# First mixer's small loads, the routing's order, narrow second blocks, and 18 chunk buffers

## The chip, the core and the metric

The kernel runs on one core of one Trainium2 chip. Time is the device time of one execution in microseconds (us); three executions of the kernel before took 1806.77, 1803.26 and 1806.77 us, median 1806.77. PE is TensorE, DVE is VectorE, ACT is ScalarE, POOL is GpSimd and SP is the engine that issues the transfers of the weights here.

## The reference, cut to what matters

Two transformer blocks follow each other on 256 tokens of width 1024 in float32. What the change touches:

```python
# first block
z = rms_norm(h, attn_norm) @ w_in                     # q, k, v, u
h = h + concat(diff_attention(q, k, v), pool_mixer(u)) @ w_out
h = h + moe(rms_norm(h, ffn_norm))                    # 32 experts, 4 for each token
h = h + sigmoid(rms_norm(h, ple_gate_norm) @ w_ple_gate) * rms_norm(p @ w_ple_proj, ple_post_norm)
# moe: logits = xn @ w_router + b_router; top 4; softmax of these; for expert e
gt = minimum(xb @ w_gate[e] + b_gate[e], 7.0); up = clip(xb @ w_up[e] + b_up[e], -7.0, 7.0)
y = ((up + 1.0) * (gt * sigmoid(1.702 * gt))) @ w_down[e] + b_down[e]
# second block: window attention and a gated recurrence, then
h = h + hierarchical_moe(rms_norm(h, norm2_w_2))      # 4 groups of 8 experts, 2 for each token
```

In the first mixture each matrix of an expert is 1024 x 1024 (4 MiB), in the second 1024 x 512. With the inputs of the reference expert 0 of the first mixture gets 73 tokens, and no other expert of it more than 64.

## The kernel before

All weights, some 655 MB, are streamed once. `specs()` lists them as chunks of 1 MiB in the order of their use, and `w_issue` (line 154) issues them from SP in that order, as soon as a buffer is free in the pools that are open: 7 buffers always (`wp`), 4 more in pool `m1_xa` from the end of the first mixer on, and 6 more in the first mixture (`NX[False] = (4, 6)`), 17 in all. A buffer comes free with `w_done`, when the last reader of its chunk has finished.

**Mixers.** A dense product takes its weights in two halves: `piece_emit` lets ACT write the rounded half `w_hi` and DVE the rest `w_lo` into a ring of four, and PE multiplies both (tile `lin`). The first mixer runs `lin_first` and three `lin_tok` (q and k, v, u), with the attention and the pool beside them, and then the product with `w_out`. `attend_pool` asks at its start for the small loads `aux`, `bands`, `wpool` and `bias_sb` (line 560), and after the second product for `wr_sb` (line 611), the two routers' matrices, which DVE multiplies by the gains. After the pool it splits the experts' biases: ACT copies `bias_sb` to `bias` (line 91) and DVE subtracts to get the lower half. In this middle part the scheduler sets the order on each engine, so these instructions don't stand where the code has them.

**Routing** (`route`, both mixtures) is written out in order. For each half of the tokens ("tile" 0 and 1) `added` adds the product to `h_res`, `squares` and `factor` give the norm's factor `rr`, `keep` writes the normed tokens in two halves, `xth` on ACT and `xtl` on DVE, `turn` transposes `h_res` into a `w_hi` room, `logits` multiplies with `wr_sb`, `choose` picks the experts on DVE (`le` to `sel`), and `place` counts them on PE (`po`). `weights` then makes the slots `posm`, the gates, and the counts `cnt`, on which the mixtures' first count loads, and so the next chunks, wait. `one_hots` makes `P`, with which `gather` collects the tokens of four (or eight) experts.

**First mixture** (`all_experts`). For each expert `gate`, `up` and `down` multiply 4 chunks each with the first 64 tokens of the expert; `product` then opens `tc.If(cnt > 64)` (line 1583), and its body `extra` does the same for the tokens 64 to 127, with tiles of 512 columns in two groups of 64. `more`, for an expert with over 128 tokens, stands at expert 24 (line 1768). The gate of the per-layer embedding has its first chunks (`w_ple_gate`, columns 0 to 511, two chunks) ahead of expert 31's `w_up`; they are split at expert 30 into four kept rooms of pool `m1_xa`. `mixer2` begins with the product of these and with the remaining `w_ple_gate`.

Of the kernel before, what the change touches and what calls it, by code (L numbers as in the profile page):

```python
# [10 lines left out]
F32 = mybir.dt.float32  # L11
# [67 lines left out]
class Prog:  # L79
# [346 lines left out]
    def specs(self):  # L426
# [34 lines left out]
        def mixture(second):  # L461
            for e in range(33):
# [16 lines left out]
        self.w_until[False] = len(s)  # L479
        cols(A["w_ple_gate"][0], 512, 1024, PK_PLE)  # L480
# [62 lines left out]
    def attend_pool(self, ph, xh, xl):  # L543

        nc, tc = self.nc, self.tc
        if True:
# [7 lines left out]
            wpool = sb.tile([128, 4, 128], F32, name="wpool")  # L554
# [85 lines left out]
            for _ in side:  # L640
                pass
            return acc
# [153 lines left out]
    def mixer2(self):  # L796
        nc, tc = self.nc, self.tc
        with ExitStack() as ph:
# [7 lines left out]
            with tc.tile_pool(name="b_ple", bufs=2, reuse_waits="tile") as gp:  # L806
                ws = self.p_q
                self.pieces_begin(sp, 29, 0)
                self.norm_tr(self.h[:, 0], 0, xh, xl)
                ss = self.small.tile([128, 2, 2], F32, name="gss")  # L810
# [24 lines left out]
                for t in range(2):  # L835
                    for n in range(4):
# [6 lines left out]
                        if t == 0 and n == 3 or t and n < 2:  # L843
                            self.piece_emit()
# [375 lines left out]
    def route(self, ph, xh, xl, accs):  # L1220
# [17 lines left out]
        def turn(t):  # L1238
            x = r["xT"][t] = self.sp.tile([128, 8, 128], F32, name="w_hi", bufs=self.AHEAD + 2)
            for k4 in range(2):  # L1240
# [4 lines left out]
                if k4:  # L1245
# [4 lines left out]
        def keep(t):  # L1250

# [3 lines left out]
            f = r["r"][:, t:t + 1]  # L1255
            self.cp(xth, xp, f)
            for i in range(2):
                at = (slice(None), slice(None), i) if k == 2 else (slice(None), i)
                self.stt(xtl[at], xp[at], f, xth[at], OP.mult, OP.subtract)
# [10 lines left out]
        def added(j):  # L1270
            add = self.res(j)

            def f(t, p):
                add(t, p)
                if t == 0:
                    squares(t, j)
                    if j:
                        factor(0)
                        keep(0)
            return f  # L1280

        with tc.manual_schedule():
# [6 lines left out]
            turn(1)  # L1289
# [599 lines left out]
```

## Time and profile before

| | |
|---|---|
| three executions | 1806.77, 1803.26, 1806.77 us, median 1806.77 |
| the profiled execution | 1803.07 us, of which the span is 1801.2 |
| busy share of the span | PE 87%, PE weight load 42%, DVE 38%, ACT 21% |
| HBM read | 655.41 MB, 364 GB/s over the span |

The stages stand in the span at about: first mixer 0 to 112 us, first route 112 to 128, first mixture 129 to 1105, embedding gate and second mixer to 1317, second route to 1348, second mixture to the end. The table of windows gives, for each stretch, the busy time of every engine and its count of instructions, then the granted clock of PE as a share of full speed, the share of time in which the 16 DMA engines were busy, and the bytes moved. A timeline has one row for each run of like instructions: start, duration, engine, line, what is written from what, and in brackets the idle time before it and what ended it.

### The profile page before, as it was taken

How to read it: one execution, taken by the hardware profiler on the slowest of the kernel's cores; microseconds unless marked ns; L12 is line 12 of the kernel's file. 1: busy time of each engine (PE TensorE's matmuls, PEld its weight loads, DVE VectorE, ACT ScalarE, POOL GpSimd, SP SyncE). 2: the span in 40 equal slices, each digit the busy share in tenths (PEclk: the TensorE clock that was granted, in tenths of full speed). 3: DMA queues.
4: the chain of work that ended last, by engine and by line, in shares of the span. 5: the costliest groups of instructions: out<-in, count | busy, mean ns of one | idle time of the engine just before them, and what ended most of it. 6: DMA issues, size and time to landing. Idle time of an engine off the chain costs nothing. (4 is left out here: it accounts for less than half of the span.)

```text
span 1801.2 us, 24529 instructions
## 1 busy us (share of the span) xinstructions
PE 1566.4 (87%) x9887; PEld 763.6 (42%) x9887; DVE 678.2 (38%) x1389; ACT 373.6 (21%) x765; POOL 25.2 (1%) x61
## 2 busy tenths in 40 slices
PE   6989999999998988989899988999979777777776
PEld 5763333333332322323233324789965433433333
DVE  4851222222322222222132334878754333323234
ACT  5631010010100100101001023786632100100100
POOL 0000000000000000000000000000000000000000
PEclk9989999999999999999899999999989977979788
DMA  9374899999999999999999997533669999999997
GB/s 349 125 297 177 328 423 424 422 423 422 424 423 424 423 424 423 423 422 424 421 424 422 424 403 307 191 121 131 242 244 404 423 424 424 424 423 423 421 424 313
DMA packets 109979, 658.88 MB, mean 366 GB/s; under 512 B 10480, under 2 KB 12400, under 8 KB 36080
## 3 DMA queue, kind: packets, MB, share of 16 engines
q1 hardware_dynamic: 108944, 655.19, 89.0%
q8 instruction: 119, 1.95, 0.4%
q10 hardware_dynamic: 720, 0.79, 0.1%
q0 software_dynamic: 144, 0.52, 0.1%
q14 instruction: 52, 0.43, 0.1%
HBM read 655.41 MB, written 1.05 MB: 364 GB/s over the span
## 5 line engine op out<-in xcount | busy, mean ns | idle before, releaser
L94 DVE TENSOR_TENSOR h_res<-h_res,cmb 128x512 f32<-128x512 f32 x260 | 167.1, 684 | 320.4 <-PE cmb L85 320.4
L85 PE MATMUL u<-wchunk,xg 128*64 128x512 f32 x1024 | 236.3, 604 | 21.6 <-DMA wchunk<-in_w_up_dram 21.5
L85 PE MATMUL g<-wchunk,xg 128*64 128x512 f32 x1024 | 250.3, 611 | 0.0
L85 PE MATMUL y<-wchunk,act_s 128*64 128x512 f32 x1024 | 236.7, 600 | 6.1 <-DMA wchunk<-in_w_down_dram 6.1
L85 PE MATMUL gu<-wchunk,xg 128*32 128x256 f32 x2048 | 181.4, 462 | 67.5 <-DMA wchunk<-in_w_up_experts_dram 39.4
L85 PEld LDWEIGHTS u<-wchunk,xg 128*64 128x64 f32 x1024 | 68.4, 138 | 169.3 <-issue 113.7
L85 PEld LDWEIGHTS gu<-wchunk,xg 128*32 128x32 f32 x2048 | 74.8, 128 | 152.4 <-DMA wchunk<-in_w_up_experts_dram 55.4
L85 PEld LDWEIGHTS y<-wchunk,act_s 128*64 128x64 f32 x1024 | 66.7, 136 | 131.1 <-issue 106.5
L91 ACT ACTIVATE yh<-y,gs 128x512 fp32r<-128x512 f32 (+1 forms) x64 | 37.2, 581 | 394.1 <-PEq L1583 286.9
L102 DVE SCALAR_TENSOR_TENSOR yl<-y,gs,yh 128x512 fp32r<-128x512 f32 (+1 forms) x64 | 39.5, 617 | 196.6 <-ACT yh L91 196.5
L85 PEld LDWEIGHTS g<-wchunk,xg 128*64 128x64 f32 x1024 | 62.9, 137 | 106.5 <-issue 95.3
L85 PE MATMUL cmb<-yh,PT 32*128 32x256 f32 (+1 forms) x384 | 75.4, 460 | 31.6 <-DVE h_res L94 30.5
L91 ACT ACTIVATE act_s<-tph 128x256 f32<-128x256 f32 x32 | 12.3, 384 | 361.5 <-PE tph L88 361.5
L85 PE MATMUL lin<-w_hi,xh 128*128 128x512 f32 (+1 forms) x192 | 77.8, 405 | 10.4 <-ACT w_hi L91 8.9
L102 DVE SCALAR_TENSOR_TENSOR w_lo<-wchunk,pk_sb,w_hi 128x512 fp32r<-128x512 f32 (+1 forms) x120 | 83.3, 729 | 9.0 <-ACT w_hi L91 8.6
L85 PEld LDWEIGHTS cmb<-yh,PT 32*128 32x128 f32 (+1 forms) x384 | 33.1, 203 | 117.5 <-DVE h_res L94 64.5
L91 ACT ACTIVATE w_hi<-wchunk,pk_sb 128x512 fp32r<-128x512 f32 (+1 forms) x120 | 77.9, 699 | 16.7 <-PE lin L85 14.1
L98 DVE TENSOR_SCALAR act_h<-u 128x512 f32<-128x512 f32 x32 | 22.1, 692 | 156.3 <-PE u L85 156.3
L85 PE MATMUL lin<-w_lo,xh 128*128 128x512 f32 (+1 forms) x192 | 75.6, 394 | 5.6 <-DVE w_lo L102 4.7
L98 DVE TENSOR_SCALAR PT<-ga,cmain 128x256 fp32r<-128x256 f32 x65 | 31.0, 477 | 121.1 <-PE ga L85 121.1
L85 PE MATMUL lin<-w_hi,xl 128*128 128x512 f32 (+1 forms) x192 | 75.5, 393 | 0.5 <-DVE xl L125 0.5
L85 PE MATMUL y<-wchunk,hT 128*32 128x256 f32 x1024 | 65.0, 385 | 10.4 <-DMA wchunk<-in_w_down_experts_dram 9.7
(386 smaller groups left out, 1923.0 us busy)
## 6 DMA issues: line engine op xcount, KB each, us to landing
wchunk<-in_w_gate_dram SPq DMA_DIRECT2D x128, 1024.0 KB, 19.7
wchunk<-in_w_up_dram SPq DMA_DIRECT2D x128, 1024.0 KB, 19.7
wchunk<-in_w_down_dram SPq DMA_DIRECT2D x128, 1024.0 KB, 19.7
wchunk<-in_w_gate_experts_dram SPq DMA_DIRECT2D x64, 1024.0 KB, 19.7
wchunk<-in_w_up_experts_dram SPq DMA_DIRECT2D x64, 1024.0 KB, 19.7
wchunk<-in_w_down_experts_dram SPq DMA_DIRECT2D x64, 1024.0 KB, 19.7
wchunk<-in_w_in_dram SPq DMA_DIRECT2D x27, 1024.0 KB, 5.4
wchunk<-in_w_out_dram SPq DMA_DIRECT2D x8, 1024.0 KB, 5.1
```

The source lines that it names most:

```text
L85: self.nc.tensor.matmul(out, lhsT, rhs, start=start, stop=stop, skip_group_check=True)
L91: self.nc.scalar.activation(out=out, in_=in_, func=AF.Copy, scale=scale)
L94: self.nc.vector.tensor_tensor(out=out, in0=a, in1=b, op=op)
L98: (eng or self.nc.vector).tensor_scalar(out=out, in0=a, scalar1=s1, scalar2=s2, op0=op0, **kw)
L102: self.nc.vector.scalar_tensor_tensor(out=out, in0=a, scalar=s, in1=b, op0=op0, op1=op1, **kw)
```

## The change

1. In the first mixer the loads of the biases and of the routers' matrices move behind the pool's matmuls, into the rooms of `bands` and `wpool`; ACT's copy, DVE's subtraction and the two multiplications move behind the attention.
2. In both routes the second tile's squares and factor come earlier, its `choose` directly after the first tile's, and its `keep` behind that: `xth` on ACT, half of `xtl` ahead of `posm`, the other half behind the one-hots. Both copies of `turn(1)` go to ACT.
3. A second block of an expert of the first mixture takes 32 tokens (64 to 95) in four groups of 32 columns and 256 wide (`quarters`), and `more` begins at 96.
4. Rows 512 to 1023 of the gate's first columns, one chunk, come behind the last `w_down`; `mixer2` splits them itself at its start.
5. The third pool of the first mixture has 7 buffers instead of 6, 18 in all; the room comes from tiles that share a name.

```diff
@@ specs
-                    cols(A["w_ple_gate"][0], 0, 512, PK_PLE)
+                    cols(A["w_ple_gate"][0, 0:512], 0, 512, PK_PLE)
                     expert(second, e, 1)
...
         self.w_until[False] = len(s)
+        cols(A["w_ple_gate"][0, 512:1024], 0, 512, PK_PLE + 4)
         cols(A["w_ple_gate"][0], 512, 1024, PK_PLE)
@@ attend_pool
-            bias = sb.tile([128, 3, 512], F32, name="bias_sb")
-            for r in range(2):
-                nc.sync.dma_start(bias[64 * r:64 * r + 64], self.A["bias"].rearrange("(j r) n -> r j n", j=3))
...
-            self.wr = self.cst.tile([128, 8, 68], F32, name="wr_sb")
-            nc.sync.dma_start(self.wr, self.A["wr"])
-            for g, a, b in ((PK_FFN, 0, 32), (PK_NORM2, 32, 68)):
-                col = self.pk[:, g:g + 8].unsqueeze(2).to_broadcast([128, 8, b - a])
-                self.tt(self.wr[:, :, a:b], self.wr[:, :, a:b], col, OP.mult)
...
-            self.cp(self.bias, bias)
-            low = self.bias[64:128]
-            self.tt(low, bias[64:128], low, OP.subtract)
+            bias = sb.tile([128, 4, 384], F32, name="bands").rearrange("p a n -> p (a n)")
+            src = self.A["bias"].rearrange("(j r) n -> r j n", j=3)
+            for r in range(2):
+                nc.sync.dma_start(bias[64 * r:64 * r + 64].rearrange("p (j n) -> p j n", j=3), src)
+            wr = sb.tile([128, 8, 68], F32, name="wpool")
+            nc.sync.dma_start(wr, self.A["wr"])
             acc = [self.lin_banks() for j in range(2)]
             for j in range(2):
                 self.lin_acc(acc[j], mh, ml, 4, 4, True, False, side)
             for _ in side:
                 pass
+            tc.keep_in_program_order(nc.scalar.activation(out=flat, in_=bias, func=AF.Copy))
+            tc.keep_in_program_order(nc.vector.tensor_tensor(out=low, in0=bias[64:128], in1=low, op=OP.subtract))
...
+                tc.keep_in_program_order(nc.vector.tensor_tensor(
+                    out=self.wr[:, :, a:b], in0=wr[:, :, a:b], in1=col, op=OP.mult))
@@ mixer2
-                self.pieces_begin(sp, 29, 0)
+                self.pieces_begin(sp, 30, 0)
                 self.norm_tr(self.h[:, 0], 0, xh, xl)
+                for _ in range(2):
+                    self.piece_emit()
+                    ws.append(self.piece(False))
...
-                        if t == 0 and n == 3 or t and n < 2:
+                        if t == 0 and n == 3 or t and n > 1:
@@ route
-                if k4:
+                if k4 and t == 0:
                     nc.vector.tensor_copy(x[:, 4 * k4:4 * k4 + 4], ps)
...
             turn(1)
+            factor(1)
             self.choose(c, r, 0)
-            for j in range(2 - len(accs), 2):
-                squares(1, j)
-            factor(1)
-            keep(1)
             self.logits(c, r, 1)
             self.place(r, 0, pp)
             self.choose(c, r, 1)
             self.place(r, 1, pp)
+            keep_high(1)
+            keep_low(1, 0)
+            c["rest"] = lambda: keep_low(1, 1)
             self.weights(c, r, pp)
@@ new
+    def quarters(self, c, x, ws, sel, part, ps):
+        ps = ps[:, 0:256]
+        q4 = [slice(32 * q, 32 * q + 32) for q in range(4)]
...
+        for w in ws:
+            for j in range(w.shape[1]):
+                lhs = x[:, k, 0] if part < 2 else x[:, j, q4[k // 2]]
+                for q, o in enumerate(q4):
+                    self.mm(ps[o], lhs, w[:, j, 256 * q:256 * q + 256], False, k == 7)
+                k += 1
@@ all_experts, gate
-            def extra(ws):
-                st["xx"] = self.gathered(c, self.one_hots(c, e, 1, 64))
-                gx = self.linear_up(c, st["xx"], 0, ws, sel, self.bias[:, 0], self.bank("ga"))
+            def extra(ws, base):
+                st["xx"] = self.gathered(c, self.one_hots(c, e, 1, base, 32), "xg32")
...
+                self.cp(st["hx", e], self.quarters(c, st["xx"], ws, sel, 0, self.bank("ga")))
@@ all_experts
-                self.w_keep = [self.xps["m1_xa"]] * 4
+                self.w_keep = [self.xps["m1_xa"]] * 2
...
-    NX = {False: (4, 6), True: (4, 5, 3)}
+    NX = {False: (4, 7), True: (4, 5, 3)}
```

What stands in a row on DVE in the first mixer, around the third block of `w_in` (a piece of the difference, - before, + now):

```order
 L94 TENSOR_TENSOR nlam<-lams 128x1
-L94 TENSOR_TENSOR wr_sb<-wr_sb,pk_sb 128x8x32
 L98 TENSOR_SCALAR nlam<-nlam 128x1
-L94 TENSOR_TENSOR wr_sb<-wr_sb,pk_sb 128x8x36
-L94 TENSOR_TENSOR bias<-bias_sb,bias 64x1536
 L102 SCALAR_TENSOR_TENSOR w_lo<-wchunk,pk_sb,w_hi 128x512 x6
```

Six lower halves of weights now follow `nlam` directly. ACT in the same place:

```order
 L91 ACTIVATE w_hi<-wchunk,pk_sb 128x512 x4
 L419 ACTIVATE lams<-lams 128x2
-L91 ACTIVATE bias<-bias_sb 128x1536
 L91 ACTIVATE w_hi<-wchunk,pk_sb 128x512 x6
```

The copy of the biases is gone from between the upper halves. At the end of the attention ACT has, before (`xh` is the attention's output, `w_hi<-ts` a turned tile of `turn`):

```order
L91 ACTIVATE xh<-ts,subln_404 128x4x128
L239 ACTIVATE sq,rss<-h_res 128x512 x2
L111 ACTIVATE rr<-rr 128x1
L112 ACTIVATE rr<-rr 128x1
L91 ACTIVATE xth<-h_res,rr 128x1024
L91 ACTIVATE w_hi<-ts 128x512 x2
L239 ACTIVATE sq,rss<-h_res 128x512 x2
```

And now:

```order
L91 ACTIVATE xh<-ts,subln_401 128x4x128
L641 ACTIVATE bias<-bands 128x1536
L239 ACTIVATE sq,rss<-h_res 128x512 x2
L111 ACTIVATE rr<-rr 128x1
L112 ACTIVATE rr<-rr 128x1
L91 ACTIVATE xth<-h_res,rr 128x1024
L239 ACTIVATE sq,rss<-h_res 128x512
L91 ACTIVATE w_hi<-ts 128x512
L239 ACTIVATE sq,rss<-h_res 128x512
L91 ACTIVATE w_hi<-ts 128x512 x2
```

The biases stand there ahead of the squares, and the second tile's squares between the copies. DVE in the second route, from the end of the first tile's choice, before:

```order
L1329 TENSOR_REDUCE sel<-oh 128x32
L94 TENSOR_TENSOR rr<-rss 128x1
L98 TENSOR_SCALAR rr<-rr 128x1
L102 SCALAR_TENSOR_TENSOR xtl<-h_res,rr,xth 128x512 x2
L102 SCALAR_TENSOR_TENSOR l_28219<-lin,rr,rw_sb 128x4
L102 SCALAR_TENSOR_TENSOR le<-lin,rr,rw_sb 128x32
```

And now, from the same place and from the end of the second choice:

```order
L1346 TENSOR_REDUCE sel<-oh 128x32
L102 SCALAR_TENSOR_TENSOR l_37982<-lin,rr,rw_sb 128x4
L102 SCALAR_TENSOR_TENSOR le<-lin,rr,rw_sb 128x32
```

```order
L1346 TENSOR_REDUCE sel<-oh 128x32
L102 SCALAR_TENSOR_TENSOR xtl<-h_res,rr,xth 128x512
L98 TENSOR_SCALAR nm<-mx 128x2
L98 TENSOR_SCALAR ng<-m_37983 128x2
L102 SCALAR_TENSOR_TENSOR posm<-po,sel 128x64
L94 TENSOR_TENSOR P<-cmain,posm 128x256 x2
L102 SCALAR_TENSOR_TENSOR xtl<-h_res,rr,xth 128x512
```

The two halves of `xtl` stood between the choices; one stands ahead of `posm` now, and one behind `P`.

## Rows read from the trace of the kernel before

**Rows 1.** Table of windows: busy us of engines, PE's clock, DMA share, GB/s.

```profile
30.00:60.00 30.00, 17.83 (x68) 13.59 (x68) 17.07 (x33) 11.89 (x19) 1.49 (x6) 0.77 0.73 234
...
90.00:120.00 30.00, 29.57 (x166) 24.74 (x164) 17.04 (x35) 13.22 (x27) 0.40 (x1) 1.00 0.74 281
...
180.00:210.00 30.00, 26.80 (x115) 9.14 (x113) 8.85 (x17) 2.28 (x4) 0.40 (x1) 0.94 0.76 302
...
300.00:1000.00 700.00, 646.37 (x2887) 219.53 (x2884) 179.62 (x323) 62.37 (x124) 9.62 (x24) 0.99 1.01 423
...
1320.00:1350.00 30.00, 18.77 (x103) 15.74 (x102) 16.65 (x55) 11.23 (x24) 0.89 (x3) 0.82 0.54 216
```

**Rows 2.** Timelines of SP, ACT, DVE and PE, first mixer: start, us, engine, line, tiles.

```profile
5.58 12.50 SPq L154 DMA_DIRECT2D wchunk<-in_w_in_dram  x6
...
24.31 3.73 SPq L560 DMA_DIRECT2D bias_sb<-in_bias_dram  x2
...
41.83 1.48 ACT L91 ACTIVATE bias<-bias_sb 128x1536 fp32r<-128x1536 f32 x1 [12.49 <-DMA bias_sb<-in_bias_dram]
...
44.69 0.43 DVE L94 TENSOR_TENSOR wr_sb<-wr_sb,pk_sb 128x256 f32<-128x256 f32 x1 [12.87 <-DMA wr_sb<-in_wr_dram]
...
45.58 1.76 DVE L94 TENSOR_TENSOR bias<-bias_sb,bias 64x1536 fp32r<-64x1536 f32 x1
...
35.73 0.39 PE L85 MATMUL lin<-w_lo,xh 128*128 128x512 f32 x1
35.95 0.39 PE L85 MATMUL lin<-w_hi,xl 128*128 128x512 f32 x1
43.98 0.79 PE L85 MATMUL lin<-w_hi,xh 128*128 128x512 f32 x1 [7.63 <-ACT w_hi L91]
...
52.15 0.40 PE L85 MATMUL lin<-w_lo,xh 128*128 128x512 f32 x1
...
59.82 1.10 PE L88 MATMUL ts<-cmain,qk 128*128 128x128 f32 x8 [1.13 <-DVE qk L94]
```

**Rows 3.** Timelines of DVE and PE, first route.

```profile
108.61 0.69 DVE L94 TENSOR_TENSOR h_res<-h_res,lin 128x512 f32<-128x512 f32 x1 [0.84 <-PE lin L85]
...
124.96 0.40 PE L85 MATMUL po<-sel,trir 128*128 128x32 f32 x1 [4.53 <-DVE sel L1329]
```

**Rows 4.** Timeline of PE: expert 0's second block, and an expert of the second mixture.

```profile
146.85 7.09 PE L85 MATMUL ga<-wchunk,xg 128*64 128x512 f32 x32 [0.47 <-DVE xg L94]
...
1358.47 3.66 PE L85 MATMUL gu<-wchunk,xg 128*32 128x256 f32 x64
```

**Rows 5.** Timeline of PE, end of the first mixture and start of the second mixer.

```profile
1088.00 1.94 PE L85 MATMUL y<-wchunk,act_s 128*64 128x512 f32 x8 [1.00 <-DMA wchunk<-in_w_down_dram]
...
1110.03 0.73 PE L85 MATMUL lin<-wchunk,xh 128*128 128x512 f32 x2 [0.25 <-ACT xh L91]
...
1113.16 1.03 PE L88 MATMUL ts<-cmain,h_res 128*128 128x128 f32 x8
```

**Rows 6.** Page, costliest groups: busy us, mean ns, idle before.

```profile
L91 ACT ACTIVATE w_hi<-wchunk,pk_sb 128x512 fp32r<-128x512 f32 (+1 forms) x120 | 77.9, 699 | 16.7 <-PE lin L85 14.1
```

**Rows 7.** Timelines of PE, ACT and DVE, second route.

```profile
1333.78 0.60 ACT L91 ACTIVATE w_hi<-ts 128x512 f32<-128x512 f32 x1 [3.87 <-PE ts L88]
...
1334.43 1.98 PE L85 MATMUL lin<-wr_sb,w_hi 128*128 128x36 f32 x16 [0.25 <-ACT w_hi L91]
...
1340.31 2.16 DVE L102 SCALAR_TENSOR_TENSOR xtl<-h_res,rr,xth 128x512 fp32r<-128x512 f32 x2 [2.64 <-ACT xth L91]
1342.37 0.22 DVE L102 SCALAR_TENSOR_TENSOR l<-lin,rr,rw_sb 128x4 f32<-128x4 f32 x1
...
1345.04 0.40 PE L85 MATMUL po<-sel,trir 128*128 128x32 f32 x1 [7.06 <-DVE sel L1329]
```

**Rows 8.** Instructions of line 1583, the branch over a second block: duration ns min/median/max.

```profile
L1583 PEldq COMPARE_BRANCH  x99: 65/216/360, 139.7 to 1101.5; - x99
```

**Rows 9.** Instructions of line 1768, the branch over `more`, the same columns.

```profile
L1768 PEldq COMPARE_BRANCH  x2: 6065/6111/6157, 873.3 to 1682.7; - x2
```

More of the change, by code (lines that the diff above doesn't have):

```diff
@@ L1250, in keep, with parts @@
         def keep(t):
+            keep_high(t)
+            for i in range(2):
+                keep_low(t, i)
+        def parts(t):
             k = 2048 // c["ff"]
@@ L1254, in keep, with keep_high, keep_low @@
             xth, xtl = (c[n][:, t].rearrange("p (c k q) -> p c k q", k=k, q=128) for n in ("xth", "xtl"))
-            f = r["r"][:, t:t + 1]
+            return k, xp, xth, xtl, r["r"][:, t:t + 1]
+        def keep_high(t):
+            k, xp, xth, xtl, f = parts(t)
             self.cp(xth, xp, f)
-            for i in range(2):
-                at = (slice(None), slice(None), i) if k == 2 else (slice(None), i)
-                self.stt(xtl[at], xp[at], f, xth[at], OP.mult, OP.subtract)
+        def keep_low(t, i):
+            k, xp, xth, xtl, f = parts(t)
+            at = (slice(None), slice(None), i) if k == 2 else (slice(None), i)
+            self.stt(xtl[at], xp[at], f, xth[at], OP.mult, OP.subtract)
         def factor(t):
@@ L1274, in f @@
                 add(t, p)
[L1275 to L1279, printed above, removed]
+                squares(t, j)
+                if t == 0 and j:
+                    factor(0)
+                    keep(0)
             return f
@@ L1371, in one_hots @@
     def one_hots(self, c, e0, ne, base, n=64):
-        P = self.scr.tile([128, 2, ne, n], FR, name="P" if ne > 1 else "PT2", bufs=2 if ne > 1 else 1)
+        P = self.scr.tile([128, 2, ne, n], FR, name="P" if ne > 1 else "PT2", bufs=2 if c["second"] and ne > 1 else 1)
         for t in range(2):
@@ L1377, in one_hots, with gather @@
         return P
-    def gather(self, c, P):
+    def gather(self, c, P, name=None):
         ne, n = P.shape[2:]
-        xg = self.scr.tile([128, 8, ne, n], F32, name=f"xg{ne}", bufs=1)
-        per = 512 // (ne * n)
+        if ne == 1 and not (name or c["second"]):
+            name = "P"
+        xg = self.scr.tile([128, 8, ne, n], F32, name=name or f"xg{ne}", bufs=1)
+        per = min(8, 512 // (ne * n))
         def banks():
             for k0 in range(0, 8, per):
-                ps = self.bank("ga").rearrange("p (k e s) -> p k e s", k=per, e=ne)
+                ps = self.bank("ga")[:, :per * ne * n].rearrange("p (k e s) -> p k e s", k=per, e=ne)
                 for i in range(per):
@@ L1583, in product @@
             with tc.If(st["cnt", e] > 64):
-                extra(keep)
+                extra(keep, 64)
             self.w_done(4)
@@ L1602, in up, with extra @@
             u = self.bank("u")
-            def extra(ws):
-                ux = self.linear_up(c, st["xx"], 0, ws, sel, self.bias[:, 1], self.bank("tph"))
-                self.act_fn(c, st["hx", e], ux, st["hx", e], room)
+            def extra(ws, base):
+                ux = self.quarters(c, st["xx"], ws, sel, 1, self.bank("tph"))
+                hx = st["hx", e]
+                self.act_fn(c, hx, ux, hx, room)
             def main(ws):
@@ L1615, in down, with extra @@
             y = self.bank("y")
[L1617 to L1621 removed]
+            def extra(ws, base):
+                PTx, gsx = self.slots(c, e, 2, base, 32)
+                pt = self.bank("tph")[:, 0:256].rearrange("p (j s) -> p j s", j=2)
+                for j in range(2):
+                    self.tr(pt[:, j], st["hx", e][:, j:256:2])
+                hx = self.scr.tile([128, 2, 128], F32, name="act_x")
+                self.nc.vector.tensor_copy(hx, pt)
+                yx = self.quarters(c, hx, ws, sel, 2, self.bank("ga"))
+                yh, yl = (self.scr.tile([128, 256], FR, name=n) for n in ("act_x", "gxm"))
+                self.split(yh, yl, yx, gsx)
+                for t in range(2):
+                    ps = [self.bank(n)[:, 0:256] for n in ("cmb", "cmb", "ga", "ga")]
+                    for n, y in enumerate((yh, yl)):
+                        for q in range(4):
+                            r = slice(32 * q, 32 * q + 32)
+                            self.mm(ps[q], PTx[r, t], y[r], n == 0, n == 1)
+                    for q in range(4):
+                        o = self.h[:, t, 256 * q:256 * q + 256]
+                        self.tt(o, o, ps[q], OP.add)
             product(e, 2, lambda ws: self.linear_down(c, hT, ws, sel, y, sides), extra)
@@ L1765, in more @@
     def more(self, c):
-        tc, most = self.tc, 32 if c["second"] else 128
+        tc, most = self.tc, 32 if c["second"] else 96
         with tc.If(self.count(c, 32, (ET.Pool,)) > most):
```

41 lines of the change are left out of this document (24 added, 17 removed).

## The prediction, made before the changed kernel ran

> **What bounds the kernel now.** I read the table of windows first, to find which stages are limited by what. From 300 to 1000 us the DMA share is 1.01 at 423 GB/s [rows 1]: the weights of the first mixture stream without a break, one chunk of 1 MiB every 1.048576 MB / 423 GB/s = 2.48 us, and TensorE has slack under them (646.4 busy of 700). Before that the stream isn't full (0.76 between 180 and 210), and it isn't at the second route (0.54 between 1320 and 1350) [rows 1]. So a microsecond is worth something in three places: ahead of about 220 us, where TensorE's work decides when chunk buffers come free; between the last chunk of the first mixture and the second mixture's stream; and in the bytes or buffers of the stream itself. Whatever starts the full stream earlier brings its end forward by as much, since nothing behind it has room to wait. The timelines of these places come next.
>
> **The first mixer's pause: -14.3 us.** ACT stands idle for 12.49 us until 41.83, at the copy of `bias`, DVE for 12.87 us until 44.69, at `wr_sb`, both ended by their own small loads [rows 2]. Behind these two stand the halves w_hi and w_lo of the next weights, so PE stops at 35.95 + 0.39 and has its next matmul at 43.98, after 7.63 us, and the eleventh after the stop only at 52.15 [rows 2]. The loads of w_in were issued from 5.58 on, and the last of them by 18.1 (5.58 + 12.50), ahead of bias_sb at 24.31 [rows 2] on the same queue; they are there long before. The change takes both instructions out of this place on both engines. Matmuls there follow each other by 0.22 to 0.23 us (35.73, 35.95), so the eleventh would start at 35.95 + 11 x 0.227 = 38.45 instead of 52.15: 13.7 us. Behind it PE waits once more, 1.13 us for `qk` of DVE at 59.82 [rows 2]. DVE loses 1.76 us of `bias` and the two multiplications of `wr_sb` ahead of that (one is 0.43), so part of this wait goes too; I take 0.6. Sum 14.3, bounds 11 (DVE's chain to `qk` is next in line and hides the rest) and 15. In the window 30 to 60 PE was busy 17.83 of 30 us at a granted clock of 0.77 of full speed [rows 1]: this is the size of what can come back.
>
> **The same work at its new place: +1 us.** ACT's copy, DVE's 1.76 and the two multiplications (0.43 and about as much) now stand between the last xl and `h_res` of the first tile. DVE waited 0.84 us there for PE [rows 3]; 1.48 on ACT and then 2.6 on DVE lie in this cover only in part, so `h_res` comes some 2.4 us later and the tile's squares, factor and keep with it. Against that stands the reordering: the second tile's choice followed ACT's xth and DVE's xtl, and PE waited 4.53 us for `sel` [rows 3]; now the choice stands ahead of them, while keep_low(1, 0) stands ahead of `posm`. The copies of turn(1) are now both on ACT, one behind the other. I count +1; bounds -1 (all the delay is covered) and +4 (nothing is gained by the choice). A wait is added on SP: the late loads of `bias` and `wr_sb` go into the tiles of the pool's bands and weights, so they stand behind the pool's last matmuls, and the chunks for the mixture queue behind them. These fill buffers that are not read before the route ends, so I price it at nothing; if one of them came late for the first products, the stream would lose a chunk, 2.5 us, which lies inside the +4.
>
> **Narrow second blocks: -10.3 us.** Only expert 0 has over 64 tokens here (73 by the reference's inputs), so one block of each product runs. Each costs PE 7.09 us for 32 records (gate at 146.85 [rows 4]; the two rows of up and down, at 163.13 and 188.11, read alike). In the new form, four groups of 32 columns and 256 wide, the same 1024 x 1024 weights are 64 records; this form is in the trace already, as gate and up of an expert of the second mixture, 3.66 us [rows 4]. Three times 3.43 is 10.3. All three stand before 200 us, where TensorE decides. The gather, the turn and the adds of the block are smaller too, and I count nothing for them; bounds 8 and 13.
>
> **The 18th buffer: -2.5 us.** One more chunk is in flight before the first buffer comes free, so the stream has one chunk less behind it: 2.48 us, if the stream is not held by PE all the way. Bounds 0 and 2.5.
>
> **The gate's weights behind the last w_down: -2.5 us.** One of the two chunks of `w_ple_gate` leaves the stream of the mixture. Near its end PE waits for chunks of w_down, 1.00 us for the one at 1088.00 [rows 5], and the end of the first mixture follows the last chunk, so it comes 2.48 us earlier. The second mixer now splits two pieces' worth itself at its start: four w_hi of 0.70 us on ACT, 2.8 us [rows 6], and as many w_lo on DVE. PE has matmuls of the ready half from 1110.03 to 1113.16 meanwhile, 3.1 us [rows 5], and these hide them; without that cover they cost up to 2.8. The sum of this part is -2.5, bounds -2.5 and +0.3.
>
> **The second route: -5.0 us.** Here the two halves xth and xtl of the second tile stand on the path: DVE's xtl at 1340.31 takes 2.16 us and waited 2.64 for ACT's xth; the choice starts at 1342.37, and PE waits 7.06 us for `sel` until 1345.04 [rows 7]. The next chunks wait for the counts behind this. In the new order the second choice can start as soon as its logits are there: PE has them at 1334.43 + 1.98 = 1336.4, and as the second copy of the turned tile now stands behind the first on ACT, one copy of 0.60 later [rows 7], at 1337.0. That is 5.4 us before 1342.37. Half of xtl, 2.16 / 2 = 1.08 us, now comes between the choice and `posm`; DVE waited there for PE's `po` anyway, so I take 0.4 of it as cost. Bounds 3 (xth on ACT ends late, and the gather waits for the second half of xtl) and 6.
>
> The rest goes together at nothing: the merged tile names, and 96 instead of 128 in `more`, which doesn't run. **Sum**: -14.3 + 1 - 10.3 - 2.5 - 2.5 - 5.0 = -33.6 us. From the profiled execution, 1803.07 us, this gives 1769.5; the median of the runs, 1806.77, lies 3.7 above it and gives 1773.2. I take 1771, between the two.
>
> **Rivals.** (A) The gain is eaten at the seams: the moved copies delay `h_res` by all of their 4 us, the mixer gives only 11, the extra split isn't hidden. That is -11 + 4 - 8 - 0 + 0.3 - 3 = -17.7, 1785 to 1789 at worst; about 1779 when half of it happens. For it: the moved work stands where PE is the limit, busy 29.57 of 30 us from 90 to 120 [rows 1]. Against: each term has its own row. Chance 0.20. (B) The narrow blocks are no cheaper, because a group of 32 columns that isn't run beside the others costs a full pass: 10.3 us are lost, 1781. Against it stands the row of the second mixture, the very form. Chance 0.07. (C) Slower: the bodies under `If` on PE grow, gate's from 49 matmuls to 68, up's from 17 to 36,, and PE jumps over them 93 times. Today a jump costs 0.22 us at the median, at most 0.36 [rows 8]. But two jumps over `more`, a very long body, cost 6.07 and 6.16 us [rows 9], so a jump's price depends on its length. PE's slack in the stream is (700 - 646.4) / (700 / 30) = 2.3 us for an expert (an expert is 12 chunks, 30 us). An expert's three jumps decide from 2.3 + 33.6 / 31 = 3.4 us of added cost. If every second expert's gate paid 6.1 us and the two others 0.5 each, 4.05 an expert, the time would be 1771 + 31 x 1.75 = 1825. What speaks for a smaller price: the bodies of before already differ by 17 to 49 in length, and their jumps lie in one narrow band; up's new body is shorter than gate's old one. Chance 0.04. The Trainium skill, page "Runtime: NRT & Kernel Launch", section "Instruction fetch mechanics", says that a taken branch out of the two instruction pages held has to fetch its target first; the rows of L1768 agree with that rule, and by it (C) is a question of where a page ends. (D) The early gain is swallowed, since the stream and not PE sets the mixture's start: then only the end terms remain, -2.5 - 2.5 - 5.0, about 1795. Against: the DMA share is 0.76 between 180 and 210 [rows 1]. Chance 0.03, and 0.02 more that nothing measurable changes.
>
> **How the numbers follow.** Forecast 0.64; with the rivals the range of 8 in 10 is 1763 (all upper bounds: -15 - 1 - 13 - 2.5 - 2.5 - 6 = -40, from 1803.07) to 1786, which takes in (B) and the better part of (A). A difference of 0.2%, 3.6 us, is about what a measurement of this kernel can tell from no change. Faster by more 0.94, within it 0.02, slower 0.04.
>
> **What would show it.** In the changed profile PE should have no gap of several microseconds before 60 us, and the granted clock of the window 30 to 60 should be near 1; the matmuls of expert 0's second blocks should stand as 64 records of 256 in about 3.6 us; the DMA share should reach 1 some 25 us earlier; PE's wait for `sel` at the second route should be about 2 us. The jumps over the bodies should stay below 0.5 us. The forecast is wrong if `h_res` of the first tile comes over 4 us late, if PE's jumps grow to microseconds, or if the stream starts earlier and loses the gain in a new wait on the way.

## The result and the profile after

The changed kernel took **1778.08 us** (median; 1775.94 to 1778.37) against 1806.53 us (1803.26 to 1806.77) of the kernel before, measured beside it: a ratio of 0.9842, with a 95% interval from 0.9828 to 0.9857. That is 28.5 us, where the forecast of 1771 meant about 35. The profiled execution of after took 1778.37 us with a span of 1776.6; that of before took 1803.07, which is the lower end of its runs. So from profile to profile only 24.6 us are seen, and all ledgers below are made in this frame.

The table of windows of after, the columns as in [rows 1]:

```profile
30.00:60.00 30.00, 30.00 (x143) 23.62 (x142) 28.46 (x68) 19.76 (x43) 3.17 (x6) 1.00 0.71 270
90.00:120.00 30.00, 22.95 (x109) 20.29 (x108) 15.90 (x45) 11.15 (x25) 2.22 (x5) 0.72 0.71 284
180.00:210.00 30.00, 28.67 (x122) 9.48 (x124) 8.94 (x19) 1.70 (x3) 0.40 (x1) 0.94 0.86 348
210.00:240.00 30.00, 28.68 (x131) 9.30 (x129) 10.07 (x18) 2.33 (x4) 0.40 (x1) 1.00 1.01 422
300.00:1000.00 700.00, 644.68 (x2879) 219.02 (x2877) 181.27 (x325) 62.34 (x126) 9.19 (x23) 1.00 1.01 421
```

The pause is gone: from 30 to 60 us PE is busy all the time at the full clock, 17.83 us and 0.77 before [rows 1]. From 90 to 120 it has become worse: the window holds the first route now, and the granted clock is 0.72. And in the stream 423 GB/s have become 421, at a DMA share of 1.01 in both. The stream has no break from about 205 us on, in before from 225 (in windows of 5 us, the last with a DMA share below 0.95 are 200 to 205 and 220 to 225): 20 us earlier, where 25 was the sign to look for.

The timeline of PE in the first route of after (start, duration, engine, line, operation, tiles; in brackets the idle time ahead and what ended it):

```profile
96.96 1.04 PE L88 MATMUL ts<-cmain,h_res 128*128 128x128 f32 x8
...
102.42 2.89 PE L85 MATMUL lin<-wr_sb,w_hi 128*128 128x32 f32 x16 [3.04 <-ACT w_hi L91]
105.12 1.95 PE L88 MATMUL ts<-cmain,h_res 128*128 128x128 f32 x8
106.90 3.62 PE L85 MATMUL lin<-wr_sb,w_hi 128*128 128x32 f32 x16
...
112.74 0.39 PE L85 MATMUL po<-sel,trir 128*128 128x32 f32 x1 [1.61 <-DVE sel L1346]
```

The wait for `sel` has shrunk from 4.53 [rows 3] to 1.61 us, but a new one of 3.04 stands ahead of it, and the matmuls behind that are slow. The timeline of ACT shows what the 3.04 are:

```profile
96.12 0.63 ACT L239 ACTIVATE sq<-h_res 128x512 f32<-128x512 f32 x1 [2.68 <-DVE h_res L94]
...
101.16 0.63 ACT L239 ACTIVATE sq<-h_res 128x512 f32<-128x512 f32 x1 [2.22 <-DVE h_res L94]
...
101.79 0.58 ACT L91 ACTIVATE w_hi<-ts 128x512 f32<-128x512 f32 x1
```

The copy `w_hi` of the first turned tile, for which PE waits, stands behind the square of the second tile, and that waits for DVE's `h_res`, which in turn comes after the moved subtraction of 1.76 us (at 92.86) and the two multiplications of `wr_sb`.

The narrow blocks of expert 0, timeline of PE, beside the 7.09 us of [rows 4]:

```profile
137.14 5.44 PE L85 MATMUL ga<-wchunk,xg 128*32 128x256 f32 x64
...
151.63 3.64 PE L85 MATMUL tph<-wchunk,xg 128*32 128x256 f32 x64
...
173.59 3.66 PE L85 MATMUL ga<-wchunk,act_x 128*32 128x256 f32 x64 [0.56 <-DVE act_x L1660]
```

Two of the three took what was forecast; the first took 5.44.

The second route, timelines of PE and DVE, beside [rows 7]:

```profile
1320.17 1.12 DVE L102 SCALAR_TENSOR_TENSOR xtl<-h_res,rr,xth 128x512 fp32r<-128x512 f32 x1
...
1320.31 0.39 PE L85 MATMUL po<-sel,trir 128*128 128x32 f32 x1 [2.21 <-DVE sel L1346]
```

PE's wait for `sel` fell from 7.06 to 2.21 us, and half of `xtl` follows the choice, as forecast.

From these timelines a **ledger** can be made: places that all kernels have (start of PE's matmuls) and how much earlier after reaches them.

| stretch of the program | before ends at | after ends at | gained, us | forecast |
|---|---|---|---|---|
| to the end of the first out projection (`ts` of `h_res`) | 112.50 | 96.96 | 15.5 | 14.3 |
| first route, to the first product of expert 0 | 131.43 | 120.19 | -4.3 | -1 |
| experts 0 and 1, to the `u` of expert 2 | 227.74 | 209.27 | 7.2 | 10.3 |
| rest of the first mixture, to the `y` of expert 31 | 1094.80 | 1075.17 | 1.2 | 5.0 (buffer 2.5, gate's chunk 2.5) |
| second mixer and second route, to its first `gu` | 1351.49 | 1327.15 | 4.7 | 5.0 |
| to the end of the span | 1801.22 | 1776.58 | 0.3 | 0 |

Sum 24.6, forecast 33.6. Three rows fall short, by 10.2 us together: the first route (3.3), experts 0 and 1 (3.1) and the mixture (3.8). The first row gained 1.2 more than forecast. The largest question is the last, since every term that I had for it is one of the stream.

### The profile page after: what moved, and what is told of

Its sections match the earlier page's. It is cut to its first block, busy times and chain, and to the rows that moved or that the text cites. A ratio compares the mean times of both kernels' runs of the same rounds, so it can differ in the third digit from the quotient of the medians.

```text
span 1776.6 us, 24734 instructions
## 1 busy us (share of the span) xinstructions
PE 1557.8 (88%) x10010; PEld 766.1 (43%) x10010; DVE 675.8 (38%) x1391; ACT 373.7 (21%) x766; POOL 27.0 (2%) x61
## 3 DMA queue, kind: packets, MB, share of 16 engines
HBM read 655.41 MB, written 1.05 MB: 370 GB/s over the span
## 5 line engine op out<-in xcount | busy, mean ns | idle before, releaser
L94 DVE TENSOR_TENSOR h_res<-h_res,cmb 128x512 f32<-128x512 f32 (+1 forms) x260 | 166.0, 680 | 319.2 <-PE cmb L85 318.2
```

Source lines behind the costliest of these rows:

```text
L94: self.nc.vector.tensor_tensor(out=out, in0=a, in1=b, op=op)
```

## The experiments

Times in each section are medians with their range; the ratio to the kernel before has its 95% interval; "u2 to y31" is the fourth row of the ledger, 867.1 us in before. The kernels were timed in four groups, each with the kernel before, whose median lay between 1804.08 and 1806.53 us; so differences of totals across sections are good to some 2 us.

### Only the narrow blocks on the kernel before

```diff
 # kernel before, part 3 alone
-                extra(keep)
+                extra(keep, 64)     # 32 tokens, four column groups (quarters)
 # ... the bodies themselves, and the rooms that some tiles share, as in the change
```

> The kernel before with the narrow second blocks alone (17 buffers, old loads, old routes, old w_ple_gate). Theory P (pages): the longer bodies under If make PE's instruction stream longer, each 16 KiB page of it is fetched through the same DMA engines as the weights, and the stream of the first mixture slips by one step of 1.0 to 1.2 us for every 8 pages; so here about 87 pages of queue q8 between 250 and 1060 us (62 before, 87 after), some 11 steps and 4 to 6 us lost in the stream, against 7.7 to 10.3 us won on TensorE at expert 0: net -2 to -6 us. Rival B (buffers): the slip after came from the 18th buffer or the shared rooms; then no slip here, 62 pages or not, and a net of -8 to -10 us. Rival C (PE's branches): no slip of DMA but PE's jumps grow; net as in B, since PE has 2.3 us of slack for an expert.

1798.05 us (1797.66 to 1801.27), ratio 0.9956 [0.9939, 0.9972]. The profile reaches `u` of expert 2 7.6 us earlier than before, and then takes 872.4 us from u2 to y31 instead of 867.1: 5.3 us of the early gain are given back inside a stretch in which only expert 0's bodies, long past, do any work. So the narrow form has a price that lies in the 31 experts that don't use it. The medians give 8 us of gain, which alone would fit the expectation's rival, that nothing is given back; the profiles give 1.7. The profiled execution of before was the fastest of its runs, the one here the slowest: it takes 89.0 us from the first product to `u` of expert 2, where the later kernels with narrow bodies for all and without a slow first block take 85.0 to 85.7. The rows compare places inside the executions, and later sections repeat the price of 5.3 from other pairs. The transfers between 300 and 1000 us (packets, MB, share of 16 engines by queue; before has 423 GB/s in that window [rows 1]):

```profile
DMA packets 40611, 295.01 MB, mean 421 GB/s; under 512 B 4485, under 2 KB 4485, under 8 KB 4869
...
q1 hardware_dynamic: 40511, 293.57, 100.4%
q8 instruction: 76, 1.25, 0.7%
```

### The second bodies for expert 0 alone

```diff
 # after
             main(self.chunks(4, keep))
-            with tc.If(st["cnt", e] > 64):
-                extra(keep, 64)
+            if e == 0:
+                with tc.If(st["cnt", e] > 64):
+                    extra(keep, 64)
```

> The changed kernel without the second blocks of experts 1 to 31 (left out; only expert 0 has over 64 tokens with these inputs, so nothing of what runs is missing). Theory P: instruction pages of q8 between 250 and 1060 us fall from 87 to about 25 to 40, the steps of the stream from 11 to 3 to 5, and the time by 6 to 9 us against the changed kernel: 1769 to 1772, ratio to before 0.979 to 0.981. Rival B or C: the stream keeps its 11 us of steps, the time changes by less than 1.5 us.

1761.41 us (1761.04 to 1764.57), ratio 0.9758 [0.9742, 0.9775]: 16.7 us faster than after by the medians, although what is left out never runs. Its transfers from 300 to 1000 us:

```profile
DMA packets 40920, 296.79 MB, mean 424 GB/s; under 512 B 4527, under 2 KB 4527, under 8 KB 4911
...
q1 hardware_dynamic: 40879, 296.24, 100.9%
q8 instruction: 26, 0.43, 0.2%
```

and those of after:

```profile
DMA packets 40612, 295.00 MB, mean 421 GB/s; under 512 B 4486, under 2 KB 4486, under 8 KB 4870
...
q1 hardware_dynamic: 40513, 293.58, 100.4%
q8 instruction: 75, 1.23, 0.7%
```

q8 carries the instructions, in packets of 1.23 MB / 75 = 16 KB. Each takes 0.7% x 16 x 700 / 75 = 1.05 us of one DMA engine. In after 49 more of them pass than here, and 2.66 MB of weights fewer, which is two and a half chunks or 6.3 us. u2 to y31 is 852.0 us here and 865.9 in after, 13.9 us less, and `u` of expert 2 comes 4.2 us earlier, 3.4 of it between the first product of expert 0 and its `u`, since this profile has no slow first block (see the section on 17 buffers). What costs is that the code is there, not that it runs. The expectation was 6 to 9 us for the whole, so it fell short; and the pages alone are not priced here: of the 13.9 us the window shows 6.3, and the branches are gone too. PE, which waits for no chunk there, goes from `u` of expert 4 to that of expert 8 in 105.7 us instead of 110.8.

### Only the late loads on the kernel before

```diff
 # kernel before, part 1 alone
-            self.cp(self.bias, bias)
+            tc.keep_in_program_order(nc.scalar.activation(out=flat, in_=bias, func=AF.Copy))
 # ... behind the out projection, as in the change
```

> The kernel before with the moved loads, bias copy, subtraction and router multiplications alone. If the pause in the first mixer was theirs, PE ends the out projection 15.5 us earlier, as in the changed kernel. Theory S (seam): the moved copies stand ahead of h_res of the first tile on DVE, so about 2.2 us come back until the first product; with the old order of choices the gain at the first product is 11 to 13 us and the time falls by as much, 1793 to 1796. Rival: the route hides the copies, then 15 us, 1791.

1792.37 us (1791.39 to 1793.26), ratio 0.9923 [0.9907, 0.994], a little below the expected range. The end of the out projection comes 15.4 us earlier, as in after. The first route takes 20.9 us from there to the first product; it took 18.9 in before and takes 23.2 in after. So the moved work costs 1.9, and what else after has, the new order of the route (part 2) above all, adds 2.4 where it was to gain. u2 to y31 is 867.0, as in before: the long bodies are not in this kernel, nor is what they cost.

### The moved work between the halves of the out projection

```diff
 # after
-            for j in range(2):
-                self.lin_acc(acc[j], mh, ml, 4, 4, True, False, side)
+            self.lin_acc(acc[0], mh, ml, 4, 4, True, False, side)
 # ... copy of bias, subtraction, multiplications of wr_sb
+            self.lin_acc(acc[1], mh, ml, 4, 4, True, False, side)
@@ route
             turn(0)
+            if len(accs) == 2:
+                squares(1, 0)
-                squares(t, j)
+                if t == 0 or j:
+                    squares(t, j)
```

> The changed kernel with the bias copy, its subtraction and the router multiplications between the two halves of the out projection instead of behind them, and the second tile's first squares behind the copies of turn(0). Theory S: of the 4.3 us that the first route lost, the 2.2 us of DVE ahead of h_res and the 0.7 us of squares ahead of the copy of turn(0) come back, and as PE then waits less than 3.04 us at the logits its granted clock may not fall to half there: first product 3 to 7 us earlier, time 1771 to 1775. Rival: the logits wait for something else, or w_lo of the out projection now waits for the 1.76 us on DVE: gain below 1 us.

1771.1 us (1769.32 to 1771.68), ratio 0.9804 [0.9788, 0.9821]: 7 us better than after by the medians. The timeline of PE:

```profile
101.37 1.86 PE L85 MATMUL lin<-wr_sb,w_hi 128*128 128x32 f32 x16
103.07 1.07 PE L88 MATMUL ts<-cmain,h_res 128*128 128x128 f32 x8
104.39 1.97 PE L85 MATMUL lin<-wr_sb,w_hi 128*128 128x32 f32 x16 [0.25 <-ACT w_hi L91]
```

The wait of 3.04 is gone, and the 2.89 and 3.62 us of after are 1.86 and 1.97 again. The route takes 16.8 us, less than before's 18.9: with its first copy free, part 2 does gain there. It isn't for nothing: the out projection ends at 99.12 instead of 96.96, as DVE's split of its next weights now stands behind the moved subtraction.

### The moved work on POOL

```diff
 # after, with the order of squares as in the kernel above
-            tc.keep_in_program_order(nc.scalar.activation(out=flat, in_=bias, func=AF.Copy))
-            tc.keep_in_program_order(nc.vector.tensor_tensor(out=low, in0=bias[64:128], in1=low, op=OP.subtract))
+            nc.gpsimd.tensor_copy(out=flat, in_=bias)
+            nc.gpsimd.tensor_tensor(out=low, in0=bias[64:128], in1=low, op=OP.subtract)
 # the multiplications of wr_sb likewise, all right behind the loads
```

> As e4_seam, but the bias copy, its subtraction and the router multiplications are done by POOL, which is idle then, as soon as the loads land. Theory: in e4_seam the out projection ended 2.2 us later than in the changed kernel because two lower halves of weights stood behind the 2.5 us of DVE; with POOL doing it this comes back, and nothing stands ahead of h_res: first product 2 us earlier than in e4_seam, time 1768 to 1770. Rival: POOL is so slow, or slows DVE beside it so much, that the biases come late or w_lo does: as e4_seam or worse.

1769.9 us (1769.65 to 1770.11), ratio 0.9811 [0.9794, 0.9827]; its ratio and that of the kernel above can't be told apart. The timeline of POOL:

```profile
77.19 1.47 POOL L636 CAST bias<-bands 128x1536 fp32r<-128x1536 f32 x1 [40.61 <-DMA bands<-in_bias_dram]
78.70 0.61 POOL L640 TENSOR_TENSOR wr_sb<-wpool,pk_sb 128x256 f32<-128x256 f32 x1
79.39 4.38 POOL L637 TENSOR_TENSOR bias<-bands,bias 64x1536 fp32r<-64x1536 f32 x1
83.86 1.54 POOL L640 TENSOR_TENSOR wr_sb<-wpool,pk_sb 128x288 f32<-128x288 f32 x1
```

The subtraction takes 4.38 us there and 1.76 on DVE, but POOL had been idle for 40 us, and it is done at 85.4, 12.5 us before the out projection ends. The out projection ends at 97.89, within a microsecond of after's, and the route takes 16.5 us. So the first route's loss lay in where things stood, not in the moving. The moved work and the second tile's square change their places together in both kernels, so what each of the two cost isn't told apart.

### 17 buffers

```diff
 # after
-    NX = {False: (4, 7), True: (4, 5, 3)}
+    NX = {False: (4, 6), True: (4, 5, 3)}
 # ... and the tile `bselx` has a room of its own again
```

> The changed kernel with 17 chunk buffers instead of 18. Theory: the 18th buffer is one chunk of the stream, 2.48 us; the chunks from number 71 on land 2.5 us later than in the changed kernel, pages of q8 and the stream's steps unchanged (86 pages, 11.6 us), time 1779.5 to 1782. Rival: TensorE holds the stream all the way to where it is full, then no difference; or 17 buffers have fewer steps, then faster.

1781.19 us (1780.09 to 1782.37), ratio 0.9875 [0.9859, 0.9892]. u2 to y31 is 869.7 us, 3.8 more than in after: the 18th buffer is worth rather more than one chunk of 2.48. And its profile shows what happened to the first narrow block:

```profile
136.21 3.66 PE L85 MATMUL ga<-wchunk,xg 128*32 128x256 f32 x64
```

The work up to there is the same as in after, where this row is 5.44. Windows of 5 us (columns as in [rows 1]), of after:

```profile
125.00:130.00 5.00, 5.00 (x27) 2.21 (x28) 0.00 (x0) 1.68 (x4) 0.00 (x0) 1.00 0.93 387
130.00:135.00 5.00, 5.00 (x35) 3.75 (x31) 0.00 (x0) 0.00 (x0) 0.00 (x0) 0.90 0.02 8
135.00:140.00 5.00, 5.00 (x43) 2.97 (x46) 0.42 (x1) 0.00 (x0) 0.00 (x0) 0.50 0.02 3
140.00:145.00 5.00, 3.99 (x47) 1.80 (x41) 0.83 (x2) 1.42 (x4) 0.00 (x0) 0.92 0.99 347
```

and of the kernel with 17 buffers:

```profile
130.00:135.00 5.00, 5.00 (x38) 3.49 (x34) 0.00 (x0) 0.00 (x0) 0.00 (x0) 1.00 0.00 0
135.00:140.00 5.00, 4.87 (x79) 2.73 (x78) 0.42 (x1) 0.07 (x1) 0.00 (x0) 1.00 0.30 88
```

In after the granted clock fell to 0.50, the level of 1.2 GHz, a second time while PE was busy without a gap; here it stayed at 1.00.

### Without the moved chunk of the gate

```diff
 # after, part 4 undone
-                    cols(A["w_ple_gate"][0, 0:512], 0, 512, PK_PLE)
+                    cols(A["w_ple_gate"][0], 0, 512, PK_PLE)
 # ... and its four kept rooms, as in before
```

> The changed kernel with the old place of the embedding gate's second chunk (two chunks ahead of expert 31's w_up, four kept rooms, split in the mixture). Theory: the last product of the first mixture starts 2.5 us later than in the changed kernel; the second mixer's start gets back the 0.7 us it lost, so time +1.5 to +2.5 us, 1779.5 to 1780.5. Rival: the end of the mixture isn't set by the last chunk, then no difference or 0.7 us faster.

1781.0 us (1778.85 to 1781.88), ratio 0.9874 [0.9857, 0.989], a little above the expected range. u2 to y31 is 868.9, 3.0 us longer than in after. From that `y` to the first `gu` of the second mixture it is 251.8 us here and 252.0 in after: what the mixer then splits itself has no price.

### The old order in both routes

```diff
 # after, part 2 undone
-            factor(1)
             self.choose(c, r, 0)
+            for j in range(2 - len(accs), 2):
+                squares(1, j)
+            factor(1)
+            keep(1)
 # ... and the copies, squares and halves of `xtl` that go with it
```

> The changed kernel with the old order of both routes (choice after keep, squares of the second tile late). Theory: at the second route 5 us are lost again; at the first route the new order was worth little or less than nothing, since DVE and PE at half clock wait for other things there: first product within 1.5 us of the changed kernel's. Time +4 to +6 us, 1782 to 1784. Rival: the new order is worth 3 us or more at the first route too, and only the moved copies cost there: then +8, 1786.

1781.31 us (1780.67 to 1785.45), ratio 0.988 [0.9864, 0.9897], a little below the expected range. The first route takes 21.4 us (23.2 in after), the second 5.4 us more than in after, from the last split of the second mixer's weights (`w_lo` on DVE) to the first `gu`. So the new order gains what was forecast in the second route and loses 1.8 in the first.

### Wide bodies again, 17 buffers

```diff
 # after, parts 3 and 5 undone
-                extra(keep, 64)
+                extra(keep)
 # ... the bodies of before, and its 17 buffers
```

> The changed kernel without narrow bodies and with 17 buffers, to be held against e5_17buf, which differs by the narrow bodies alone. Theory: TensorE takes 10.5 to 11.5 us longer over expert 0 (three products of 7.09 instead of 3.66 us, and the gather's and adds' smaller parts), and the stream gets 6 us back (60 pages instead of 85): the narrow bodies as a whole are worth only 4 to 6 us, time 1785 to 1788. Rival: their whole 10 us: 1791 or more.

1787.66 us (1787.23 to 1788.06), ratio 0.9894 [0.9872, 0.9917]. u2 to y31 is 864.4; it was 869.7 with the narrow bodies and as many buffers. From the first product to `u` of expert 2 it takes 97.4 us, and its first block is slow too, at a granted clock of 0.66 from 135 to 140 us:

```profile
135.93 8.78 PE L85 MATMUL ga<-wchunk,xg 128*64 128x512 f32 x32 [0.47 <-DVE xg L94]
```

### A narrow body for expert 0, the wide ones for the others

```diff
 # after, with the moved work on POOL
             def extra(ws, base):
-                st["xx"] = self.gathered(c, self.one_hots(c, e, 1, base, 32), "xg32")
+                if e >= 1:
+                    st["xx"] = self.gathered(c, self.one_hots(c, e, 1, base, 64), "xgx")
 # ... the wide body of before; for these experts `more` begins at 128
+                    return
+                st["xx"] = self.gathered(c, self.one_hots(c, e, 1, base, 32), "xgx")
```

> As e8_seam_pool with 18 buffers, but only expert 0 has the narrow body; experts 1 to 31 have the old one (64 slots in two groups of 64 columns, 512 wide, `more` from 128 for them). With these inputs no body but expert 0's runs, so TensorE's work that runs is that of e8 to the last matmul; only instructions that are jumped over differ. Theory P: pages of q8 between chunks 71 and 386 fall from 86 to about 62, the stream's excess over 2.48 us a chunk from 11.5 to 5 to 6 us, the time by 6 us: 1762.5 to 1765. Rival C (nothing but what runs counts): as e8, 1769 to 1770.5.

**1764.03 us** (1762.69 to 1765.79), ratio 0.9765 [0.9745, 0.9784]. It computes everything for any count of tokens (that expert 0 is the one with the narrow body follows the reference's inputs), and beats both kernels: before by 2.35%, after by about 14 us. Against the kernel with the moved work on POOL it differs in the bodies of experts 1 to 31, which never run here, and in the rooms that some tiles share: more of them do here, so shared rooms are not what the narrow bodies cost. Both start alike, timeline of PE in this kernel (`u` of experts 2, 4 and 11, `y` of expert 31):

```profile
199.49 0.47 PE L88 MATMUL u<-bias,bsel 128*128 128x512 f32 x1 [0.16 <-PEq L1625]
...
256.59 0.48 PE L88 MATMUL u<-bias,bsel 128*128 128x512 f32 x1 [0.16 <-PEq L1625]
...
447.88 0.47 PE L88 MATMUL u<-bias,bsel 128*128 128x512 f32 x1 [0.16 <-PEq L1625]
...
1060.72 0.50 PE L88 MATMUL y<-bias,bsel 128*128 128x512 f32 x1 [0.60 <-DVE yl L105]
```

and in the one with narrow bodies for all:

```profile
199.45 0.47 PE L85 MATMUL u<-bias,bsel 128*128 128x512 f32 x1 [0.16 <-PEq L1622]
...
256.57 0.47 PE L85 MATMUL u<-bias,bsel 128*128 128x512 f32 x1 [0.16 <-PEq L1622]
...
447.87 0.48 PE L85 MATMUL u<-bias,bsel 128*128 128x512 f32 x1 [0.16 <-PEq L1622]
...
1065.53 0.50 PE L85 MATMUL y<-bias,bsel 128*128 128x512 f32 x1 [0.60 <-DVE yl L102]
```

4.85 us lie between the first and the last of these places, and none of it between the middle two, 191.3 us in both: there PE waits for no chunk in either kernel, so its own pace decides, and the jumps over the longer bodies don't slow it. The transfers of the hybrid from 300 to 1000 us are at 423 GB/s again:

```profile
DMA packets 40770, 295.97 MB, mean 423 GB/s; under 512 B 4505, under 2 KB 4505, under 8 KB 4889
...
q1 hardware_dynamic: 40693, 294.90, 100.6%
q8 instruction: 54, 0.88, 0.5%
```

## Why the prediction came out as it did

**u2 to y31 taken apart.** The twelve kernels give this stretch for eight combinations of the three parts:

| second bodies of experts 1 to 31 | buffers | chunk of the gate | u2 to y31, us | kernels |
|---|---|---|---|---|
| wide | 17 | in the mixture | 867.1, 867.0 | before, late loads only |
| narrow | 17 | in the mixture | 872.4 | narrow blocks only |
| wide | 17 | behind it | 864.4 | wide bodies again |
| narrow | 17 | behind it | 869.7 | 17 buffers |
| narrow | 18 | in the mixture | 868.9 | without the moved chunk |
| narrow | 18 | behind it | 865.9 to 866.3 | after, old order, both seams |
| wide | 18 | behind it | 861.2 | hybrid |
| none | 18 | behind it | 852.0 | bodies for expert 0 alone |

Pairs that differ in one column give the narrow bodies +5.3 (twice) and +4.9, the 18th buffer -3.2, -3.5 and -3.6, the gate's chunk -2.7, -2.7 and -2.8. After has all three: 5.3 - 3.5 - 2.8 = -1.0, measured -1.2.

**The step that failed** is "The rest goes together at nothing", with rival (C) behind it: the longer bodies under `If` were priced only as jumps of PE's sequencer, and those indeed stayed small. Line 1620 of after, which answers to [rows 8], in the same columns:

```profile
L1620 PEldq COMPARE_BRANCH  x99: 65/327/460, 129.0 to 1083.0; - x99
```

The median rose from 216 to 327 ns, the maximum from 360 to 460, far from microseconds. But the code of the bodies that are jumped over is brought into the core all the same, in pages of 16 KB (75 of them between 300 and 1000 us in after, 26 where experts 1 to 31 have no body), by the same 16 DMA engines that carry the weights. Where these have no free time, a page takes its place from the stream: between after and the hybrid 21 more of them (75 against 54, 0.35 MB) between 300 and 1000 us, and 1.32 MB of weights fewer, which is 3.1 us at 423 GB/s, or 0.15 us for a page; over u2 to y31 4.9 us. PE's longer jumps are not the cause: where PE sets the pace, 21 of them cost nothing that can be seen (191.3 us in both kernels above), and the DMA engines have no more free time with the longer bodies, q1 and q8 taking 101.1% together in after as in the hybrid. A page costs two to three times its share of the engines (1.05 / 16 = 0.066 us). The rest seems to lie in the weights' own packets: from the same rows (share x 16 x 700 us / packets) one took 277.6 ns in after and 276.9 in the hybrid, which is 1.7 us over 40513 packets on 16 engines, beside 21 x 0.066 = 1.4 us for the pages themselves. The shares are rounded, so this is rough, and why these packets take longer stays open.

The Trainium skill, page "Runtime: NRT & Kernel Launch", section "Instruction fetch mechanics", says that instructions are streamed in blocks of 16 KiB over a DMA queue of their own, and that crossing into the next block is mostly hidden. The size agrees with the rows of q8. That it is hidden doesn't hold in this kernel while the stream is full. I had read that section for the jumps alone.

Point by point:

- **The first mixer's pause**: right, 15.5 where 14.3 was forecast and 15 was the bound. From 15 us to the end of the out projection PE has one wait, of 0.9 us, and the full clock.
- **The moved work, +1**: mis-sized, +4.3, just past its upper bound of +4. The cover of DVE's 0.84 us of waiting was counted and the squares of the second tile were not: set ahead of the copy on which PE waits, they passed the lateness of `h_res` on to it. With late loads alone it is +1.9, with the new order +4.3, and with the work on POOL and the square behind the copy -2.5. Part of the loss is the clock, which was 0.50 from 105 to 110 us, behind the wait of 3.04, so that the routers' products took 2.89 and 3.62 us; those of before took 1.87 and 1.97, ahead of its own fall to 0.54 from 120 to 125.
- **The narrow blocks, -10.3**: right for what runs. From the first product to `u` of expert 2 the kernel with 17 buffers needs 85.7 us, 10.7 less than the 96.3 of before; after's own profile has 7.2 less, as the clock fell during the first block. (Against the 97.4 of the kernel with wide bodies and as many buffers it is 11.7, but 1.7 of that is the slow first block there, 8.78 us instead of 7.09.) Without that fall on either side the term stands at 10.0 to 10.7. The fall is not a cost of the narrow form: the wide first block met it in two profiles, the narrow one in two. Which executions meet it wasn't settled.
- **The 18th buffer, -2.5**: 3.2 to 3.6, above the bound of one chunk that I gave it; why it is more than a chunk stays open.
- **The gate's chunk, -2.5**: right, 2.7. The splits have become 124 instead of 120 [rows 6], and the four more, at the start of the second mixer, are hidden as argued.
- **The second route, -5.0**: right, 5.4 between the last split of the second mixer's weights and the first `gu` (29.7 us in before, 24.2 in after). The ledger's 4.7 also holds the mixer, 0.6 to 0.7 us longer up to that split, without the moved chunk of the gate too.

So the direction and four terms held; of the 9 us that are missing in the ledger 5 are the pages and 6 the first route and the clock, with 2 gained beyond the forecast in the mixer and the buffer. Rival (A) had the right place for one of these, and (C) the right part of the code with the wrong mechanism. That the time still lies in the range is in part luck: the range was made wide for (A) and (B), and a cost that it didn't foresee fitted into it.

## What to carry to other kernels

Code that is jumped over had a price here, where the DMA engines were full: count the instructions of every unrolled body, not only of those that run, and keep a rarely taken body short or specialize it to the iterations that are known to need it (here known from the reference's inputs alone). When work is moved out of a wait, look at what stands behind its new place on the in-order queue, down to the instruction that the critical engine waits for; an idle engine that is slower at it (POOL here) can be the better place. And a stretch between two places that all variants share separates effects of a few microseconds that total times, which vary by as much, would not.

## What was not expected of the hardware

- One 16 KB packet of instructions took about 1.05 us of a DMA engine; 21 more of them in 700 us went with 3.1 us less of weights, 49 more with 6.3.
- Expert 0's first narrow block met a granted clock of 0.50 in two profiles (after: 5.44 us, narrow blocks only: 5.37) and 1.00 in seven (3.66). In after PE was busy without a gap before and during the fall. The wide block met it in two (late loads only: 8.69, wide bodies again: 8.78) and not in before (7.09).
- The rise of the jump's median with the body's length is small (216 to 327 ns), while `more`, much longer, still takes 6.0 to 6.3 us on PE's sequencer in after, as in [rows 9].
